# Squares for the residual stream's norms: added over the feature chunks on GpSimd, and one ones-product

## The chip, the cores and the metric

The kernel runs on one core of one Trainium2 chip. The core has TensorE (PE, matrix products into PSUM), VectorE (DVE), ScalarE (ACT) and GpSimd (POOL), which work on SBUF side by side and wait for each other by semaphores, and DMA queues. The metric is device time in microseconds; the kernel before takes 3798.35 us, the median of three runs from 3797.68 to 3798.63.

## The reference

The reference computes three blocks one after the other on 512 latent tokens of 1024 features, beside which the first block has 256 context tokens. The first block has two layers. The change touches these two layers alone, and in them one thing: the mean square in the norms that read the residual stream `x`.

```python
def rmsnorm(u, g):
    uf = u.astype(jnp.float32)
    y = uf * lax.rsqrt(jnp.mean(uf * uf, axis=-1, keepdims=True) + EPS)
    return (y * g.astype(jnp.float32)).astype(u.dtype)
...
        hl = modulate(rmsnorm(xl, g_pre_mix[i]), ml[0], ml[1])
...
        xl_new = xl + ml[2] * rmsnorm(y_l, g_post_mix[i])
        h2 = modulate(rmsnorm(xl_new, g_pre_mlp[i]), ml[3], ml[4])
        xl_new = xl_new + ml[5] * rmsnorm(sqrelu_mlp(h2, w_mlp_in[i], w_mlp_out[i]), g_post_mlp[i])
```

In each layer a mixer (latent attention, a gated convolution, a short convolution) and an MLP add their normed outputs to `x`, and `x` is normed again ahead of the next product. The context goes the same way in the first layer. A second attention block and a layer of experts that are looked up by keys follow; they stay as they are.

## The kernel before

The stream is kept with the features on the partitions: eight chunks of 128 features, each a tile of 128 x 768 columns, 256 of the context (`xc`) and 512 latent (`x`). Weight products are done in three parts (`mm3`, L322), since every fp32 value is split into a high and a low part (`hh`, `hl` for the tokens; `wh` made by ACT in L276 and `wl` by DVE in L277 for the weights). A product's result goes to PSUM in tiles of two kinds: `a` (`acc`, 1024 columns, two of them) and `b` (`acc1`, 512 columns, four of them); the units of `lin` take the two kinds in turn.

A norm needs the mean over the features, which lie on the partitions. A product with a matrix of ones, divided by 1024, gives it on all partitions (`ones_mean`, L345, and L568). An fp32 product is two passes on TensorE. `rstd` (L333 and L334 on ACT, L335 and L336 on DVE) makes the reciprocal root from the PSUM tile, and `prenorm` (L532 on DVE, L533 on ACT, L534 on DVE) makes the normed tokens of each chunk, as `hh` and `hl`, which the next products read.

`chain` adds a normed output to the stream: for each of the eight chunks DVE multiplies (L547) and adds (L550), ACT squares the new `x` (L565) and `meansq_x` adds that square's column sums to the PSUM tile (L568). Then `prenorm` follows, or the sum is kept. `meansq_x` is also called for the input, in `build` and `start`. There are eleven such sums up to 1726 us, each of a range of columns: set 1 (512 columns, the input's first tokens, in `build`), set 2 (256, the input's others, in `start`), sets 3 (512) and 4 (256) behind the mixer of layer 0, sets 5 to 7 (256 each) behind its MLP, and sets 8 and 9 (256 each) and 10 and 11 (256 each) behind the mixer and the MLP of layer 1.

The chains are generators that run in steps beside the products. Beside them the modulation of the layers is computed in groups of 256 columns: L467 multiplies `mraw` or `mg` (from DMA) with `cs` into a `b` tile, ACT copies it to `mrow` (L469), L472 turns it, and L474 and L476 on DVE finish it. The order on each engine is set by a scheduler from the order in which the code is written and the tiles that are taken: a tile of a kind that has been taken later can only come into use behind those taken before it.

Of the kernel before, what the change touches and what calls it, by code (L numbers as in the profile page):

```python
# [5 lines left out]
F32 = mybir.dt.float32  # L6
# [3 lines left out]
OP = mybir.AluOpType  # L10
# [61 lines left out]
TBW = 16  # L72
# [171 lines left out]
class K:  # L244
# [26 lines left out]
    def split(self, raw, shape):  # L271
        """hi, lo of raw"""
        nc = self.nc
        hi = self.t("wh", shape, F32R, NWH, self.wp)
        lo = self.t("wl", shape, F32R, NWH, self.wp)
        nc.scalar.copy(hi, raw)  # L276
        nc.vector.tensor_tensor(lo, raw, hi, op=OP.subtract)  # L277
        return hi, lo
# [6 lines left out]
    def take(self, key, hold=False):  # L285
        """the next weights of the plan, the ones behind them on their way; held ones stay until they are dropped"""
        if not self.ready:
            self.ready.append((self.plan[0][0], self.plan.popleft()[1]()))
        k, w = self.ready.popleft()
        assert k == key, (k, key)  # L290
        self.held += hold
        self.refill(not hold)
        return w
# [5 lines left out]
    def drop(self, w):  # L299
        """a held one that is used for the last time"""  # L300
        self.held -= 1
        self.refill(1)
        return w
# [13 lines left out]
    def mm3(self, outs, w, x, start, stop):  # L317
        """outs: psum aps; w: (hi, lo) stationary; x: per out (hi, lo) moving."""
        nc = self.nc
        for xi, wi in ((0, 0), (1, 0), (0, 1)):  # L320
            for o, xx in zip(outs, x):
                nc.tensor.matmul(o, w[wi], xx[xi], start=start and xi == 0 and wi == 0, stop=stop and wi == 1)  # L322

# [1 line left out]
    def ct(self, tag, w):  # L325
        """a temporary tile of the norms between the parts of a layer"""
        return self.t("PTq", [128, 512], F32, 6)[:, :w]

    def rstd(self, mean_ps, n, t=None):
        """mean_ps: psum [128, n] of mean squares on all partitions; -2 / sqrt of them, to be used with gains times -1/2"""  # L330
        nc = self.nc
        v, y = (t(x, n) if t else self.t(x, [128, T])[:, :n] for x in ("rs_v", "rs_y"))
        nc.scalar.activation(y, mean_ps, AF.Abs_reciprocal_sqrt, bias=self.eps)  # L333
        nc.scalar.activation(v, y, AF.Square)  # L334
        nc.vector.scalar_tensor_tensor(v, mean_ps, EPS, v, op0=OP.add, op1=OP.mult)  # L335
        nc.vector.scalar_tensor_tensor(y, v, 3.0, y, op0=OP.subtract, op1=OP.mult)  # L336
        return y

    def ones_mean(self, src, n, dim):
        """mean over features of src [128, n] (sum over partitions / dim), as psum [128, n]"""  # L340
        p = self.acc1() if n <= 512 else self.acc()
        o = self.ones[dim]
        for a in range(0, n, 512):
            b = min(a + 512, n)
            self.nc.tensor.matmul(p[:, a:b], o, src[:, a:b], start=True, stop=True)  # L345
        return p[:, :n]
# [17 lines left out]
    def setup(self):  # L364
# [4 lines left out]
        # gains times -1/2, the weights of the gated convolution times 1/2  # L369
# [26 lines left out]
    def load_xc(self):  # L396
        """the context's tokens, three feature chunks to a tile"""
        self.xc = []
        for i in range(0, 8, 3):
            t = self.t("xc", [128, T])  # L400
            for k in range(i, min(i + 3, 8)):
                c = t[:, (k - i) * SC:(k - i) * SC + SC]
                self.nc.sync.dma_start(out=c, in_=self.a["cT"][k])
                self.xc.append(c)

    def xa(self, k, c0, c1):
        """columns c0 to c1 of feature chunk k; the context's tokens come first"""
        return self.xc[k][:, c0:c1] if c1 <= SC else self.x[k][:, c0 - SC:c1 - SC]

    def pipe(self, tasks):  # L410
        """tasks in order; a task that yields n goes on behind the n-th task after it"""
# [22 lines left out]
    def adv(self, n=1000):  # L434
        """n steps of the first of the generators that run beside the tasks"""
        while n and self.bg:
            if next(self.bg[0], self) is self:
                self.bg.popleft()
                return
            n -= 1  # L440
# [20 lines left out]
    def mod_group(self, l, g, ws):  # L461
        """columns 256 g to 256 g + 256 of the modulation of layer l"""
# [15 lines left out]
    def mods(self, todo):  # L478
        """closures for the groups (layer, group) of todo; a group's weights are loaded behind the group before it"""

        def step(i):
            ws = self.mw or self.mod_load(*todo[i])
            self.mod_group(*todo[i], ws)
            self.mw = self.mod_load(*todo[i + 1]) if i + 1 < len(todo) else None

        return [lambda i=i: step(i) for i in range(len(todo))]

    def tick(self, upto=1000):
        """one more group of modulations, upto that many in all"""
# [4 lines left out]
    def mod_fold(self, l, j, gname, plus_one, k0, k1):  # L494
        """[128, k1 - k0, 2]: -gain / 2 * (mod_j (+1))"""
# [9 lines left out]
    def fold(self, l, j, gname, plus_one, k):  # L505
        """column of mod_fold for feature chunk k, made for two chunks at a time"""
# [9 lines left out]
    def pieces(self, r):  # L516
        """(stream, first column, last column) of a range of columns"""
        return [(s, max(r[0], a), min(r[1], b)) for s, a, b in ((1, 0, SC), (0, SC, T)) if r[0] < b and r[1] > a]

    def prenorm(self, l, j, gname, mean, hs, rg):  # L520
        """normed and modulated tokens of columns rg as hi, lo; yields after each chunk"""
# [15 lines left out]
    def chain(self, l, j, gname, Y, ssq, nxt, hs, rg):  # L537
        """x += gate * norm(Y) and the norm that follows, on the tokens of columns rg"""
# [19 lines left out]
    def meansq_x(self, p, k, rg):  # L558
        """mean square over the features of the tokens, added up in psum"""
# [3 lines left out]
        s = self.ct("sqt", w)  # L563
        for _, a, b in self.pieces(rg):
            nc.scalar.activation(s[:, a - x0:b - x0], self.xa(k, a, b), AF.Square)  # L565
        if k == 0:
            p = self.acc1()
        nc.tensor.matmul(p[:, :w], self.ones[1024], s, start=k == 0, stop=k == 7)  # L568
        return p if k < 7 else p[:, :w]

    def lin(self, ap, hs, R, w=None, ks=None):
        """products of a tile of 128 columns: one psum tile for each range of R"""
# [18 lines left out]
    def stagger(self, units, hs, stages, n, upto):  # L591
        """units on the ranges of the first stage, then on those of the next ones, with n steps beside each"""
# [12 lines left out]
    def start(self, units, hs):  # L605
        """the first units, on the first tokens as they become ready, then on the others"""
# [32 lines left out]
    def normed_hilo(self, c, r, g, n, dst=None):  # L639
        """c * g * r as hi, lo"""  # L640
# [4 lines left out]
    def layer(self, l, hs):  # L645
# [11 lines left out]
        # ---- conformer branch  # L657
# [66 lines left out]
        # ---- short convolution branch  # L724
# [43 lines left out]
        # ---- latents, keys and queries  # L768
# [73 lines left out]
        def k_pair(i):  # L842
            """keys of heads 2 i and 2 i + 1: the second one's rows lie the other way round"""
# [30 lines left out]
        # ---- attention of two heads on a block of 128 queries  # L874
# [62 lines left out]
        # ---- output projection  # L937
# [28 lines left out]
        # the first units run on the tokens that are ready  # L966
# [36 lines left out]
        # ---- mlp  # L1003
# [77 lines left out]
    def norm2(self, gname, X, mean):  # L1081
        """normed tokens as hi, lo, from the mean squares in psum of each range of columns"""
# [25 lines left out]
    def stackq(self, out, z, e, w=slice(0, S)):  # L1108
        """head e of z: hi on its own rows of out, lo on the other ones"""
# [4 lines left out]
    def stackk(self, z):  # L1114
        """each head of z twice on top of itself"""
# [6 lines left out]
    def mm64(self, out, q, k, stop=True):  # L1122
        """q: hi and lo of 64 rows on top of each other; k: hi twice, lo twice"""
# [13 lines left out]
    def lin2k(self, key, hs, wide=False):  # L1137
        """products of the plan's next tile of weights"""
# [7 lines left out]
    def block2(self):  # L1146
# [10 lines left out]
        # the halves of the rotary rows change places here; the other rows stay zero  # L1157
# [4 lines left out]
        def rope_unit(j, gi, done):  # L1162
            """a tile of 128 columns (two heads): norm, gain and rotary, then done"""
# [45 lines left out]
        # ---- values and gates, token-major  # L1209
# [29 lines left out]
        # ---- compressed keys and values  # L1239
# [112 lines left out]
        # ---- selected and window branches: head pair i (heads i and 4 + i) on query block qb  # L1352
# [18 lines left out]
        def out(key, qb, Y, tag):  # L1371
            """psum of the pair of query blocks of qb, and a copy of it behind the second"""
# [50 lines left out]
        # ---- dilated attention: head pair jp on query block qb  # L1423
# [86 lines left out]
        # ---- merge  # L1510
# [56 lines left out]
        at = {}  # L1567
# [32 lines left out]
    def peer(self, hs):  # L1600
# [44 lines left out]
        def route(b):  # L1645
            """experts and weights of token block b, pairs on partitions; yields the vector engine's ns"""
# [29 lines left out]
            # row and column of the candidate  # L1676
# [34 lines left out]
        def weights(tb, share):  # L1711
            """expert weights of TBW tokens; each share-th group of four on the vector engine only"""
# [27 lines left out]
        def routing():  # L1740
            """expert weights of a token block beside the routing of the next one; yields the ns on the vector and the scalar engine"""
# [59 lines left out]
    def build(self, upto=None):  # L1801
# [18 lines left out]
        def feed(i):  # L1820
            """modulation and norm of the first tokens for two more chunks of features"""
# [48 lines left out]
```

## Time and profile before

| | |
|---|---|
| median of three runs | 3798.35 us (3797.68 to 3798.63) |
| profiled execution, span | 3799.5 us, 52788 instructions; the page gives no other time for it |
| TensorE busy | 3700.0 us, 97% |
| VectorE, ScalarE busy | 2464.8 us (65%), 1749.5 us (46%) |
| GpSimd busy | 159.3 us, 4%, most of it in the last third |

The page gives busy time for each engine, the clock that TensorE was granted, and the chain of work that ended last, followed back from the last instruction. The groups by line give busy time, the mean of one in ns, and the idle time ahead of them with what ended it. The timeline and the table by stretch give the same for any stretch. A pair of passes that stands in a full queue is drawn longer than it costs, because the ends of products are modelled; what it costs is the distance to the next start.

### The profile page before, as it was taken

The numbers are of one execution on the slowest core, as the hardware profiler recorded it, in microseconds if no ns is written. First come the engines' busy times: TensorE is split into PE (matmuls) and PEld (weight loads), VectorE is DVE, ScalarE is ACT, GpSimd is POOL, SyncE is SP. The second block draws the span as 40 slices with busy tenths as digits, with TensorE's granted clock in tenths as the row PEclk, the third lists the DMA queues.
The fourth block names the chain that finished last, engine by engine and source line by source line (L and its number), as shares of the span: only waits on it lengthen the run. The fifth ranks groups of instructions, "written<-read, shape, count | busy, mean of one in ns | idle before, by whom it ended". The sixth has DMA issues, their size and how long they took to land.

```text
span 3799.5 us, 52788 instructions
## 1 busy us (share of the span) xinstructions
PE 3700.0 (97%) x19762; PEld 3052.0 (80%) x19762; DVE 2464.8 (65%) x4950; ACT 1749.5 (46%) x3452; POOL 159.3 (4%) x317
## 2 busy tenths in 40 slices
PE   8998999999999999999999999999999999999999
PEld 5867788888877878887778878778888888888887
DVE  5966644444788655555776568999666855555554
ACT  5256531111446732233565544767777743322232
POOL 0000000000000000000001100000000011111110
PEclk9999999999999999999999999999999999999999
DMA  6430331222341233334331233455555565665553
GB/s 209 129 106 12 122 117 62 61 66 63 105 147 51 67 117 95 94 97 138 115 99 62 93 111 106 156 168 176 178 178 178 195 218 189 201 205 187 190 186 114
DMA packets 155248, 490.28 MB, mean 129 GB/s; under 512 B 18368, under 2 KB 24832, under 8 KB 150768
## 3 DMA queue, kind: packets, MB, share of 16 engines
q1 hardware_dynamic: 128368, 374.48, 30.9%
q0 software_dynamic: 26624, 112.43, 8.7%
q8 instruction: 156, 2.56, 0.3%
q14 instruction: 100, 0.82, 0.1%
HBM read 408.86 MB, written 74.71 MB: 127 GB/s over the span
## 4 chain that ended last, share of the span: by engine, by line
PE 85%; DVE 9%; ACT 2%; DMA 2%; issue 1%; SPq 0%; POOL 0%; ACTq 0%; DVEq 0%; POOLq 0%
PE b L322 56%; PE a L322 19%; PE b L917 2%; DVE wl L277 1%; PE b L467 1%; PE a L1732 1%; PE b L568 1%; PE b L906 1%; PE b L1419 1%; PE b L1365 1%; DMA mraw<-in_wmod_dram 1%; DVE gst L1736 1%; PE a L1125 0%; PE b L1507 0%; PE b L1174 0%
## 5 line engine op out<-in xcount | busy, mean ns | idle before, releaser
L276 ACT CAST wh<-raw 128x1024 fp32r<-128x1024 f32 (+2 forms) x531 | 547.3, 1031 | 1365.7 <-PE b L322 811.3
L322 PE MATMUL b<-hs,wh 128*128 128x512 f32 x2624 | 823.6, 395 | 4.4 <-ACT hs L1092 4.4
L277 DVE TENSOR_TENSOR wl<-raw,wh 128x1024 fp32r<-128x1024 f32 (+2 forms) x531 | 635.7, 1198 | 171.7 <-ACT wh L276 159.1
L322 PE MATMUL b<-hid,wh 128*128 128x512 f32 x2048 | 630.7, 389 | 0.0
L322 PEld LDWEIGHTS b<-hs,wh 128*128 128x128 f32 x2624 | 487.5, 190 | 107.7 <-ACT hs L1092 5.3
L322 PE MATMUL b<-hs,wl 128*128 128x512 f32 x1312 | 516.2, 393 | 1.1 <-DVE wl L277 1.1
L322 PEld LDWEIGHTS b<-hid,wh 128*128 128x128 f32 x2048 | 384.4, 188 | 80.2 <-DVE hid L1795 0.3
L322 PE MATMUL b<-hid,wl 128*128 128x512 f32 x1024 | 398.3, 389 | 0.0
L322 PE MATMUL b<-hh,wh 128*128 128x256 f32 (+1 forms) x1160 | 364.7, 351 | 3.7 <-DVE V L840 2.2
L322 PE MATMUL a<-hh,wh 128*128 128x512 f32 (+1 forms) x1144 | 354.7, 348 | 9.5 <-DVE y L1046 7.2
L322 PE MATMUL b<-hl,wh 128*128 128x256 f32 (+1 forms) x1160 | 356.3, 344 | 0.3 <-DVE hl L534 0.3
L322 PE MATMUL b<-hh,wl 128*128 128x256 f32 (+1 forms) x1160 | 355.7, 344 | 0.0
L322 PE MATMUL a<-hh,wl 128*128 128x512 f32 (+1 forms) x1144 | 350.2, 344 | 1.5 <-DVE wl L277 1.5
L322 PE MATMUL a<-hl,wh 128*128 128x512 f32 (+1 forms) x1144 | 349.9, 343 | 0.3 <-DVE hl L534 0.3
L322 PEld LDWEIGHTS b<-hs,wl 128*128 128x128 f32 x1312 | 248.4, 189 | 53.7 <-DVE wl L277 1.5
L322 PEld LDWEIGHTS b<-hh,wh 128*128 128x128 f32 x1160 | 200.5, 189 | 44.0 <-issue 4.7
L322 PEld LDWEIGHTS a<-hh,wh 128*128 128x128 f32 x1144 | 197.0, 188 | 44.3 <-issue 14.0
L322 PEld LDWEIGHTS b<-hl,wh 128*128 128x128 f32 x1160 | 201.0, 189 | 30.5 <-issue 1.2
L322 PEld LDWEIGHTS b<-hid,wl 128*128 128x128 f32 x1024 | 192.2, 188 | 39.9
L322 PEld LDWEIGHTS a<-hl,wh 128*128 128x128 f32 x1144 | 197.3, 188 | 31.8 <-issue 2.5
L322 PEld LDWEIGHTS b<-hh,wl 128*128 128x128 f32 x1160 | 200.4, 189 | 27.7 <-issue 1.1
L322 PEld LDWEIGHTS a<-hh,wl 128*128 128x128 f32 x1144 | 196.9, 188 | 30.3 <-DVE wl L277 2.3
(412 smaller groups left out, 5424.1 us busy)
## 6 DMA issues: line engine op xcount, KB each, us to landing
raw<-in_w_dram SPq DMA_DIRECT2D x134, 512.0 KB
raw<-in_pu_dram SPq DMA_DIRECT2D x128, 512.0 KB
raw<-in_pv_dram SPq DMA_DIRECT2D x128, 512.0 KB
raw<-in_win_dram SPq DMA_DIRECT2D x64, 512.0 KB
G<-gst POOLq DMA_DIRECT2D x32, 1024.0 KB, 4.9
gt<-G POOLq DMA_DIRECT2D x16, 2048.0 KB, 13.9
mraw<-in_wmod_dram SPq DMA_DIRECT2D x82, 384.0 KB
GA<-ga SPq DMA_DIRECT2D x121, 256.0 KB
```

The costliest lines, as they stand in the source:

```text
L276: nc.scalar.copy(hi, raw)
L277: nc.vector.tensor_tensor(lo, raw, hi, op=OP.subtract)
L322: nc.tensor.matmul(o, w[wi], xx[xi], start=start and xi == 0 and wi == 0, stop=stop and wi == 1)
L467: nc.tensor.matmul(p[j:j + 32, 0:256], self.cs[:, k, :], ws[k], start=k < 4, stop=k >= 4, tile_position=(0, j))
L568: nc.tensor.matmul(p[:, :w], self.ones[1024], s, start=k == 0, stop=k == 7)
L906: nc.tensor.transpose(p[:, j * 128:j * 128 + 128], Ps[e][:, kc * 128:kc * 128 + 128], self.eye)
L917: nc.tensor.matmul(o[pr, c % 2 * 128:c % 2 * 128 + 128], V[i][:, kc, pr], PT[e * nkb + kc], start=kc == 0, stop=kc == nkb - 1, tile_positi ...
L1365: nc.tensor.transpose(p[:, j * 128:j * 128 + 128], src, self.eye)
L1419: nc.tensor.matmul(o[row], V[kb][:, 128 * b + 64 * g:128 * b + 64 * g + 64], PT[kb][2 * g + b], start=False, stop=kb == qb and b == 1, til ...
L1732: nc.tensor.matmul(p[:, i * 256:i * 256 + 256], A[:, i], W[:, i].rearrange("p j e -> p (j e)"), start=True, stop=True)
L1736: nc.vector.tensor_tensor(gst[:, :, t8:t8 + 4].rearrange("p e t -> p t e"), q[:, :, 0], lo, op=OP.add)
```

## The change

`meansq_x` no longer sends each square to TensorE. The square of chunk 0 is written to a new tile, `msq` (two of them in SBUF), and stays there. The squares of chunks 1 to 7 are written as before and GpSimd adds each to `msq`. Behind the last one `ones_mean` takes a PSUM tile and multiplies `msq` with the ones once. The callers are as they were. (The diff also takes out docstrings and comments, which are left out here.)

```diff
-    def meansq_x(self, p, k, rg):
+    def meansq_x(self, acc, k, rg):
         nc = self.nc
         x0, x1 = rg
         w = x1 - x0
-        s = self.ct("sqt", w)
+        s = self.t("msq", [128, 512], F32, 2)[:, :w] if k == 0 else self.ct("sqt", w)
         for _, a, b in self.pieces(rg):
             nc.scalar.activation(s[:, a - x0:b - x0], self.xa(k, a, b), AF.Square)
         if k == 0:
-            p = self.acc1()
-        nc.tensor.matmul(p[:, :w], self.ones[1024], s, start=k == 0, stop=k == 7)
-        return p if k < 7 else p[:, :w]
+            return s
+        nc.gpsimd.tensor_tensor(acc, acc, s, op=OP.add)
+        return acc if k < 7 else self.ones_mean(acc, w, 1024)
```

The 88 products of L568 (176 passes) become eleven of L345 (22 passes), and GpSimd gets 77 additions, 63 of 256 columns and 14 of 512. In the changed kernel the additions have the line L568.

The order of TensorE in set 9 before, from the end of an `a` unit on; `b_12352` is the sum, `b_12460` a modulation group, `b_12481` a unit of 24 products:

```order
L322 MATMUL a_12550<-hh_10607,wl_12383 128x256
L568 MATMUL b_12352<-PTq_12350,ones_77 128x256
L467 MATMUL b_12460<-mraw_12333,cs 32x256 x3
L322 MATMUL b_12481<-hh_11541,wh_12260 128x256
L322 MATMUL b_12481<-hl_11542,wh_12260 128x256
L568 MATMUL b_12352<-PTq_12357,ones_77 128x256
L467 MATMUL b_12460<-mraw_12335,cs 32x256 x3
L568 MATMUL b_12352<-PTq_12363,ones_77 128x256
L467 MATMUL b_12460<-mraw_12337,cs 32x256 x2
L322 MATMUL b_12481<-hh_11541,wl_12261 128x256
L322 MATMUL b_12481<-hh_11547,wh_12260 128x256
```

The same place now; `b_12444` is the sum:

```order
L322 MATMUL a_12550<-hh_10607,wl_12381 128x256
L345 MATMUL b_12444<-msq_12350,ones_77 128x256
L467 MATMUL b_12460<-mraw_12333,cs 32x256 x3
L467 MATMUL b_12460<-mraw_12335,cs 32x256 x3
L467 MATMUL b_12460<-mraw_12337,cs 32x256 x2
L322 MATMUL b_12481<-hh_11541,wh_12260 128x256
L322 MATMUL b_12481<-hl_11542,wh_12260 128x256
L322 MATMUL b_12481<-hh_11541,wl_12261 128x256
L322 MATMUL b_12481<-hh_11547,wh_12260 128x256
```

The one product of the sum stands where the first of eight stood, and the modulation group and the unit, which stood between the eight, stand behind it. Set 4 has the same form.

VectorE in set 9 before, from chunk 5 on; L474 and L476 finish the modulation group `b_12460`, L335 reads the sum:

```order
L547 TENSOR_TENSOR PTq_12428<-y_11803,PTq_12342 128x256
L474 TENSOR_REDUCE mod_118<-b_12460 128x4
L550 SCALAR_TENSOR_TENSOR x_103<-PTq_12428,mf_12014,x_103 128x256
L476 TENSOR_TENSOR mod_118<-mod_118,vec 128x4
L547 TENSOR_TENSOR PTq_12434<-y_11843,PTq_12342 128x256
L502 TENSOR_TENSOR mf_15016<-mod_118,vecn 128x4
L550 SCALAR_TENSOR_TENSOR x_104<-PTq_12434,mf_12063,x_104 128x256
L547 TENSOR_TENSOR PTq_12440<-y_11883,PTq_12342 128x256
L550 SCALAR_TENSOR_TENSOR x_105<-PTq_12440,mf_12063,x_105 128x256
L1012 TENSOR_SCALAR pn_t_12506<-b_12481 128x256
L335 SCALAR_TENSOR_TENSOR PTq_12446<-b_12352,PTq_12446 128x256
```

The same place now, from chunk 6 on:

```order
L547 TENSOR_TENSOR PTq_12432<-y_11843,PTq_12342 128x256
L550 SCALAR_TENSOR_TENSOR x_104<-PTq_12432,mf_12061,x_104 128x256
L547 TENSOR_TENSOR PTq_12438<-y_11883,PTq_12342 128x256
L550 SCALAR_TENSOR_TENSOR x_105<-PTq_12438,mf_12061,x_105 128x256
L335 SCALAR_TENSOR_TENSOR PTq_12446<-b_12444,PTq_12446 128x256
L336 SCALAR_TENSOR_TENSOR PTq_12447<-PTq_12446,PTq_12447 128x256
L532 SCALAR_TENSOR_TENSOR PTq_12452<-x_98,mf_12117,PTq_12447 128x256
L532 SCALAR_TENSOR_TENSOR PTq_12456<-x_99,mf_12117,PTq_12447 128x256
L532 SCALAR_TENSOR_TENSOR PTq_12511<-x_100,mf_12162,PTq_12447 128x256
L534 SCALAR_TENSOR_TENSOR hl_11542<-PTq_12452,mod_118,hh_11541 128x256
L534 SCALAR_TENSOR_TENSOR hl_11548<-PTq_12456,mod_118,hh_11547 128x256
L474 TENSOR_REDUCE mod_118<-b_12460 128x4
```

The reduction L474, which stood between the chunks of the set, stands behind L335, L336 and the first steps of the prenorm.

## Rows read from the trace of the kernel before

**Rows 1.** Page: busy time by engine, and the chain by line.

```profile
PE 3700.0 (97%) x19762; PEld 3052.0 (80%) x19762; DVE 2464.8 (65%) x4950; ACT 1749.5 (46%) x3452; POOL 159.3 (4%) x317
...
PE b L322 56%; PE a L322 19%; PE b L917 2%; DVE wl L277 1%; PE b L467 1%; PE a L1732 1%; PE b L568 1%; PE b L906 1%; PE b L1419 1%; PE b L1365 1%; DMA mraw<-in_wmod_dram 1%; DVE gst L1736 1%; PE a L1125 0%; PE b L1507 0%; PE b L1174 0%
```

**Rows 2.** Groups by line on TensorE, 0 to 1730 us; columns as in part 5.

```profile
L568 PE MATMUL b<-PTq,ones 128*128 128x256 f32 (+1 forms) x176 | 65.5, 478 | 16.3 <-ACT PTq L565 16.1
```

**Rows 3.** Table by stretch, L568 alone: length, busy us (passes) of TensorE, weight loads, clock.

```profile
10.00:20.00 10.00, 9.27 (x16) 3.75 (x16) 1.00 0.98 316
...
1700.00:1713.00 13.00, 3.82 (x12) 1.80 (x12) 1.00 0.26 82
```

**Rows 4.** Timeline of set 9: start, us, engine, line, operation [idle before <- releaser].

```profile
1345.51 0.70 PE L568 MATMUL b<-PTq,ones 128*128 128x256 f32 x2
...
1350.82 0.17 DVE L474 TENSOR_REDUCE mod<-b 128x4 f32<-128x16 f32 x1 [1.77 <-PE b L472]
...
1353.26 0.42 ACT L565 ACTIVATE PTq<-x 128x256 f32<-128x256 f32 x1 [0.44 <-DVE x L550]
...
1353.77 0.28 PE L322 MATMUL b<-hl,wh 128*128 128x256 f32 x1
...
1353.89 0.59 PE L568 MATMUL b<-PTq,ones 128*128 128x256 f32 x2
...
1354.13 0.47 PE L322 MATMUL b<-hh,wl 128*128 128x256 f32 x1
...
1354.43 0.28 PE L322 MATMUL b<-hh,wh 128*128 128x256 f32 x1
...
1354.52 0.47 ACT L333 ACTIVATE PTq<-b,eps 128x256 f32<-128x256 f32 x1 [0.84 <-PE b L568]
...
1356.44 0.44 PE L472 MATMUL b<-cst,mrow 128*128 128x128 f32 x2 [0.49 <-ACT mrow L469]
...
1357.68 0.38 PE L322 MATMUL b<-hh,wh 128*128 128x256 f32 x1 [0.80 <-ACT hh L533]
```

**Rows 5.** L547 and L550 on VectorE: duration ns min/median/max, first and last start.

```profile
L547 DVE TENSOR_TENSOR PTq<-y,PTq x72: 415/419/689, 424.0 to 1724.4; 128x256 f32<-128x256 f32 x64, 128x512 f32<-128x512 f32 x8
...
L550 DVE SCALAR_TENSOR_TENSOR x<-PTq,mf,x x64: 474/483/489, 425.1 to 1724.8; 128x256 f32<-128x256 f32 x64
```

**Rows 6.** Timeline, TensorE ahead of set 6.

```profile
1022.01 0.55 PE L322 MATMUL a<-hh,wh 128*128 128x256 f32 x1 [7.24 <-DVE y L1046]
```

**Rows 7.** Table by stretch behind that idle time; the granted clock stands after POOL.

```profile
1022.00:1024.00 2.00, 1.99 (x7) 1.75 (x7) 1.93 (x6) 0.84 (x2) 0.00 (x0) 0.50 0.09 37
1024.00:1026.00 2.00, 2.00 (x12) 1.81 (x12) 1.93 (x5) 0.84 (x2) 0.00 (x0) 0.71 0.00 0
```

**Rows 8.** Groups by shape on GpSimd, two memsets.

```profile
L1160 POOL MEMSET rot<- 128x512 f32 x4 | 1.9, 543 | 0.0
...
L393 POOL MEMSET cs<- 128x256 f32 x1 | 0.3, 330 | 0.0
```

**Rows 9.** Timeline, sets 4 and 11.

```profile
466.99 0.59 PE L568 MATMUL b<-PTq,ones 128*128 128x256 f32 x2
...
471.17 0.17 DVE L474 TENSOR_REDUCE mod<-b 128x4 f32<-128x16 f32 x1 [1.58 <-PE b L472]
...
475.13 0.59 PE L568 MATMUL b<-PTq,ones 128*128 128x256 f32 x2
...
1725.89 0.70 PE L568 MATMUL b<-PTq,ones 128*128 128x256 f32 x2 [0.16 <-ACT PTq L565]
```

**Rows 10.** Chain of waits in sets 1 and 2: start us, us, what.

```profile
16.54 8.81 DMA mg<-in_wmod_dram
...
52.32 3.63 PE b L568 x16
```

**Rows 11.** Timeline of VectorE in set 4, and beside GpSimd's memsets.

```profile
477.64 1.28 DVE L532 SCALAR_TENSOR_TENSOR PTq<-x,mf,PTq 128x256 f32<-128x256 f32 x3
...
1728.50 1.28 DVE L1091 SCALAR_TENSOR_TENSOR t<-x,vecn,ry 128x256 f32<-128x256 f32 x3
```


## The prediction

> **What bounds the kernel now.** I read the page first. TensorE is busy for 97% of the span and the chain that ended last is made of weight products: L322 has 75% of it, and the lines that the change removes, L568, have 1%, about 38 us [rows 1]. Then the groups by line up to 1730 us, after which the change touches nothing: L568 is 176 matmul passes, 65.5 us, a mean of 478 ns, with 16.3 us of idle ahead of them, nearly all for ACT's squares [rows 2]. (The longest of these waits is that for the first square at the start of the kernel.) Eighty-eight pairs are eleven sums of eight, which I call sets 1 to 11 in order of time. The table by stretch gives a set 3.8 to 9.3 us of TensorE; the largest and the smallest of its eleven rows stand in the group [rows 3]. Last I read one set, number 9, row by row [rows 4], and then the prices.
>
> What a pair costs TensorE is read in set 9. Its last pair starts at 1353.89, the next product at 1354.13 and the one behind it at 1354.43, where a product without a pair behind it takes 0.12 us, as the one at 1353.77 does: 1354.43 - 1353.89 - 0.12 = 0.42 us [rows 4]. The change removes seven of eight pairs, 7 x 0.42 = 2.9 us of a set of 256 columns.
>
> **What the change does to the order.** This is the part that I think decides. Before, the sum's PSUM tile `b` is taken at chunk 0, and the eight pairs stand between other work in `b` tiles, so TensorE does that work while DVE and ACT make the next square. After, the tile is taken at the end. All later `b` tiles stand behind it, and the one L345 pair stands where the first of the eight stood, ahead of the modulation group L467 and the unit `b_12481`. TensorE comes to it when chunk 0 is done and has to wait for chunk 7 and its add. The work that filled that time comes afterwards.
>
> Set 9, worked out. TensorE reaches the sum at 1345.51, as the `a` unit ahead stands where it stood [rows 4]. The last square starts at 1353.26 and lasts 0.42 us, so it ends at 1353.68 [rows 4, 5]. DVE's reduction L474 waited 1.77 us for TensorE in the middle of the set, and goes behind the set in the new order: 1353.68 - 1.77 = 1351.9 [rows 4]. Add one addition (0.76, below): 1352.7. The stall is 1352.7 - 1345.5 = 7.2 us, against 2.9 us saved: +4.3. Some of it comes back: the norm behind the sum (L333) starts at 1352.9 in place of 1354.5, 1.6 us earlier, and runs beside the displaced products, where before TensorE idled 0.49 us ahead of L472 and 0.80 us for L533 [rows 4]; I count 1.6 + 1.3 less 0.1 as coming back. Net +1.5.
>
> The clock comes on top. TensorE's granted clock fell to half (1.2 of 2.4 GHz) while it idled 7.24 us before 1022.01, stood at 0.50 from 1022 to 1024 and at 0.71 from 1024 to 1026 [rows 6, 7]. That is 2 x 0.5 + 2 x 0.29 = 1.6 us lost behind an idle time as long as set 9's stall. Set 9: +1.5 + 1.6 = +3.1.
>
> **An addition on GpSimd.** No two-input GpSimd operation is in this trace. The near rows are memsets: 330 ns for 128x256 and 543 ns for 128x512 [rows 8]. They write only. The difference, 0.213 us, goes to 256 columns, and 0.330 - 0.213 = 0.117 is fixed. An addition reads two and writes one; with three accesses one after another it takes 0.117 + 3 x 0.213 = 0.76 us for 256 and 0.117 + 6 x 0.213 = 1.40 for 512. Bounds are one memset (0.33, 0.54) and three (0.99, 1.63). I take 0.76 and 1.40. DVE's pair of operations sets the pace of a set of 256 columns, 0.42 + 0.48 = 0.90 us of busy time [rows 5], so at 0.76 GpSimd keeps up and only the last addition shows. At 0.99 it would fall behind: some 1.1 us more in each of six sets, +6.6. At 0.33: -0.4 x 6 = -2.4.
>
> The Trainium skill, GPSIMD Engine Reference, section 3.1 Elementwise — side-by-side cycle accounting, gives about 2.6 cycles an element for a two-input add, which would be about 0.6 us at 256 columns; no row here shows one. By it the sum would be about 2 us lower.
>
> **The other sets.** Set 4: the first pair is at 466.99, the last at 475.13, and L474 cost DVE 1.58 us in between [rows 9]. Six products of 512 columns that stood behind the first pair now stand ahead, 1.4 us at about 0.23 us each. TensorE waits from 468.4 to 475.13 - 1.58 + 0.76 = 474.3, 5.9 us, against 2.9 saved; 1 us comes back through the earlier norm: +2.0. Set 7 has the same form with a stall of about 4.5 us: +1.2. Sets 5, 6, 8 and 10: a whole `a` unit is pulled ahead of the sum, so the wait is about what is saved: 0 each, +-2. Set 11: nothing stands beside it; the chain is DVE, ACT, pair, and the last pair is at 1725.89 [rows 9]. The last addition with its hop comes into the chain in place of nothing: +0.9. Set 3: DVE is the engine that paces; the last addition of 1.40 goes on its chain, less what ACT's queue cost there: +1.2. Set 2: squares straight from the input, no DVE work; sixteen passes take 3.63 us of the chain [rows 10], and seven additions of 0.76 take 5.3. The prenorm behind it is on the chain, so +1.5. Set 1: a load of the modulation weights ends at 25.35, well behind the sum [rows 10]; the additions, and a first-use delay of some us if there is one, hide there: 0.
>
> Sum: 0 + 1.5 + 1.2 + 2.0 + 0 + 0 + 1.2 + 0 + 3.1 + 0 + 0.9 = +9.9 us.
>
> **DVE beside the additions.** Three L1091 that run beside L1160's memsets take 1.28 us, as three L532 of the same shape do with GpSimd still [rows 11]. That is for a GpSimd that reads nothing. The lower bound is 0. The upper bound is that each addition keeps DVE's two-input operations out for its whole length: 7 x 0.76 = 5.3 us in each of sets 4, 6, 7, 9 and 11 and 7 x 1.40 = 9.8 in set 3, 36 us. I take a clash of one addition in seven, 5 x 0.76 + 1.40 = 5.2 us, near the row.
>
> Total +15.1 on the profiled span of 3799.5 us, so 3814.6; that span is 1.15 us over the median of the timed runs, 3798.35, so 3813 us. Between the extremes of the near terms (add at 0.33 with no clash; add at 0.99) it runs from 3803 to 3824.
>
> **Rivals.**
> *DVE is kept out.* Each addition starts as its square lands, just as DVE runs its next pair of two-input operations, so they always meet, and the one that comes second waits for the whole of the other. With the upper end of 36 us that is 3799.5 + 9.9 + 36 - 1.15 = 3844; with two thirds of it (24), as some additions fall into DVE's own waits, 3832. Against it: the memset rows. For it: no row shows a reading GpSimd beside DVE. It decides if L547 and L550 grow beyond 0.6 us in sets 3 to 11. The Trainium skill, SBUF — State Buffer, section "Who interferes with whom", states this rule: a DVE instruction with two SBUF inputs contends with a GpSimd instruction that reads SBUF, and the loser waits for the whole instruction. The rows of before neither show nor exclude it, since their GpSimd operations only write; this is why I give it over 0.2.
>
> *TensorE gains.* If the waits at the sum are short, because TensorE comes to it late or other work is found, seven sets of 256 columns (4 to 10) give 7 x 2.9 = 20 us: 3778; half of it 3788. For it: TensorE is busy 97% [rows 1], and L568 waits rarely outside the start. Against it: the order of sets 4 and 9, which I can read.
>
> *A wash.* Stalls equal what is saved and the additions hide: 3796 to 3803. It needs the displaced work to cover the norm behind the sum wholly, in every set.
>
> **Chances.** Forecast 0.50 (3803 to 3824), DVE kept out 0.22, TensorE gains 0.15, a wash 0.13. A measurement of this kernel tells about 0.2% from no change, 7.6 us, so faster is under 3790.8 and slower over 3806. Faster: most of the gain, 0.13. Same: the wash, the rest of the gain and the low end of the forecast, 0.24. Slower: 0.63. The range runs from half the TensorE gain, which it leaves out, to most of the DVE case: 3791 to 3838.
>
> **What would show it.** In the new trace L345 of sets 4, 7 and 9 has idle of 4 to 8 us ahead of it, released by GpSimd's `msq`, and TensorE's busy time to 1730 us is about 55 us lower with the same or a later end. The granted clock behind set 9 falls. Additions take 0.6 to 0.9 us. L547 and L550 stay at 0.42 and 0.48 but for single longer ones; if most are longer, the second price was wrong and the first rival holds. If the waits ahead of L345 are under 2 us, the order argument is wrong.

## The result and the profile after

The changed kernel takes 3846.67 us, the median of four runs (3844.03 to 3849.45), beside 3798.01 us for the kernel before: a ratio of 1.0127, 95% interval 1.0113 to 1.0142. It is 49 us slower. 3813 was forecast and 3838 was the end of the range.

The page of the kernel after, its span, its busy times and the chain by line:

```profile
span 3847.6 us, 52630 instructions
...
PE 3664.8 (95%) x19608; PEld 3029.0 (79%) x19608; DVE 2487.7 (65%) x4950; ACT 1755.0 (46%) x3454; POOL 241.6 (6%) x394
...
PE b L322 55%; PE a L322 18%; PE b L917 2%; DVE wl L277 1%; PE b L467 1%; PE a L1732 1%; PE b L906 1%; PE b L1419 1%; DVE PTq L547 1%; DVE x L550 1%; PE b L1365 1%; DMA mraw<-in_wmod_dram 1%; PE b L345 1%; POOL msq L568 1%; PE b L1507 1%
```

TensorE is busy for 35 us less than before, 3664.8 against 3700.0 [rows 1], and the span is 48.1 us longer. L568 and L345 alone do not stand for that in the chain: VectorE's L547 and L550, which were not among its costly lines before, have 1% each now.

TensorE's waits up to 1790 us (in total, times, the longest):

```profile
PE b L345 <- POOL msq L568: 84.2, 11, 18.9
PE a L322 <- DVE wl L277: 21.0, 3, 10.5
```

The first is the pair of the sum, eleven waits. The one at the start of the kernel is 18.9 us, where the first wait was 10.4 before; the other ten make 65 us. The second is nearly new (1.5 us before): weight halves that VectorE makes later than before.

The additions, and the two operations of VectorE that make the new stream, by shape (busy us, mean ns of one):

```profile
L568 POOL TENSOR_TENSOR msq<-msq,PTq 128x256 f32<-128x256 f32 x63 | 59.3, 941 | 1200.5 <-ACT PTq L565 1199.0
...
L568 POOL TENSOR_TENSOR msq<-msq,PTq 128x512 f32<-128x512 f32 x14 | 22.9, 1634 | 229.7 <-ACT PTq L565 229.2
```

```profile
L550 DVE SCALAR_TENSOR_TENSOR x<-PTq,mf,x 128x256 f32<-128x256 f32 x64 | 40.2, 634 | 0.7
...
L547 DVE TENSOR_TENSOR PTq<-y,PTq 128x256 f32<-128x256 f32 x64 | 33.4, 529 | 0.1
...
L550 DVE SCALAR_TENSOR_TENSOR xc<-PTq,mf,xc 128x256 f32<-128x256 f32 x16 | 13.9, 874 | 0.2
```

An addition of 256 columns takes 0.94 us on average. The mean of L550 has gone from 482 to 634 ns, and from 483 to 874 for the context's chunks, that of L547 from 419 to 529 ([rows 5] has the durations of before). The median of L550 on `x` stays at 484 ns: 24 of the 64 took more than 600 ns, and most of the others are as before. How this looks is best seen in set 9, on all engines (start, us, engine, line, operation):

```profile
1380.35 0.72 POOL L568 TENSOR_TENSOR msq<-msq,PTq 128x256 f32<-128x256 f32 x1 [1.01 <-ACT PTq L565]
1380.47 0.89 DVE L550 SCALAR_TENSOR_TENSOR x<-PTq,mf,x 128x256 f32<-128x256 f32 x1
...
1381.95 1.71 POOL L568 TENSOR_TENSOR msq<-msq,PTq 128x256 f32<-128x256 f32 x2 [0.87 <-ACT PTq L565]
1382.13 0.95 DVE L547 TENSOR_TENSOR PTq<-y,PTq 128x256 f32<-128x256 f32 x1
...
1383.12 0.83 DVE L550 SCALAR_TENSOR_TENSOR x<-PTq,mf,x 128x256 f32<-128x256 f32 x1
...
1386.62 0.42 ACT L565 ACTIVATE PTq<-x 128x256 f32<-128x256 f32 x1 [1.31 <-DVE x L550]
1387.18 0.72 POOL L568 TENSOR_TENSOR msq<-msq,PTq 128x256 f32<-128x256 f32 x1 [0.93 <-ACT PTq L565]
1387.95 1.22 PE L345 MATMUL b<-msq,ones 128*128 128x256 f32 x2 [9.33 <-POOL msq L568]
1389.10 1.94 PE L467 MATMUL b<-mraw,cs 128*32 128x256 f32 x16
1389.21 0.47 ACT L333 ACTIVATE PTq<-b,eps 128x256 f32<-128x256 f32 x1 [2.17 <-PE b L345]
```

The addition of 1380.35 takes 0.72 us, and L550, which was issued inside it, takes 0.89 and ends 0.29 us behind it. So 0.19 of its 0.48 us had passed when the addition was over, if it ran on at its usual pace; whether this is its own start or part of its work, no run shows. At 1381.95 two additions stand beside L547 at 0.95 us and L550 at 0.83, which are lengthened too. TensorE waits 9.33 us for the last addition and starts the pair 0.77 us after that addition began. Before, the first pair of this set started without a wait [rows 4]. The stretches around it (length, busy us of the engines, then TensorE's granted clock):

```profile
1384.00:1388.00 4.00, 0.05 (x1) 0.05 (x1) 2.46 (x4) 1.23 (x3) 2.35 (x3) 0.50 0.00 0
1388.00:1392.00 4.00, 4.00 (x26) 2.02 (x27) 1.69 (x5) 1.58 (x4) 0.00 (x0) 0.63 0.18 36
```

The clock was 0.50, half of full speed (1.2 of 2.4 GHz), at the end of the wait, and 0.63 over the next 4 us. It is not set 9 alone. Over the stretch up to 1790 us, before and after, the means (after POOL) are:

```profile
0.00:1790.00 1790.00, 1719.70 (x10262) 1413.25 (x10262) 1093.44 (x2077) 708.41 (x1260) 15.64 (x63) 0.98 0.31 98
...
0.00:1790.00 1790.00, 1635.62 (x9708) 1347.85 (x9709) 1099.49 (x2052) 701.13 (x1246) 92.87 (x128) 0.96 0.30 94
```

By the clock's records in the two traces it stood at 0.50 for 58 us of this stretch before and for 130 us after; TensorE was busy in 45 and in 65 us of these.

Where the 48 us came from, by the start of L333 (or of the DMA behind set 11) in both traces:

| behind | before | after | later by | of it in this stretch | forecast, without the 5.2 us of clashes |
|---|---|---|---|---|---|
| sets 1, 2 | 420.17 | 423.45 | 3.3 | 3.3 | 1.5 |
| sets 3, 4 | 992.29 | 1013.55 | 21.3 | 18.0 | 3.2 |
| sets 5 to 7 | 1103.99 | 1138.47 | 34.5 | 13.2 | 1.2 |
| (no set) | 1306.11 | 1338.73 | 32.6 | -1.9 | 0 |
| sets 8, 9 | 1698.32 | 1738.25 | 39.9 | 7.3 | 3.1 |
| sets 10, 11 | 1727.14 | 1775.46 | 48.3 | 8.4 | 0.9 |

Every group lost more than was forecast, sets 3 and 4, where the additions have 512 and 256 columns, the most.

### The profile page after: what moved, and what is told of

The parts are those of the page before. It is cut to its first block, busy times and chain, and to the rows that moved or that the text cites. A ratio compares the mean times of both kernels' runs of the same rounds, so it can differ in the third digit from the quotient of the medians.

```text
span 3847.6 us, 52630 instructions
## 1 busy us (share of the span) xinstructions
PE 3664.8 (95%) x19608; PEld 3029.0 (79%) x19608; DVE 2487.7 (65%) x4950; ACT 1755.0 (46%) x3454; POOL 241.6 (6%) x394
## 4 chain that ended last, share of the span: by engine, by line
PE 84%; DVE 10%; ACT 3%; DMA 2%; issue 1%; POOL 1%; SPq 0%; ACTq 0%; DVEq 0%; POOLq 0%
PE b L322 55%; PE a L322 18%; PE b L917 2%; DVE wl L277 1%; PE b L467 1%; PE a L1732 1%; PE b L906 1%; PE b L1419 1%; DVE PTq L547 1%; DVE x L550 1%; PE b L1365 1%; DMA mraw<-in_wmod_dram 1%; PE b L345 1%; POOL msq L568 1%; PE b L1507 1%
```

## The experiments

Four causes were to be told apart: the place of the pair in TensorE's queue (ORDER), VectorE kept out by GpSimd's additions (PORT), the time and delay that additions bring whoever makes them (LENGTH), and, against all, the gain on TensorE. Ratios are to the kernel before on the same chip, with their 95% interval; differences in us are those of medians. The kernels were not all timed on one chip, so a difference between two of them that stand beside different runs of the kernel before is less sure than a ratio.

**Pairs left out, the tile opened at chunk 0.**

```diff
-        nc.tensor.matmul(p[:, :w], self.ones[1024], s, start=k == 0, stop=k == 7)
+        if k in (0, 7):
+            nc.tensor.matmul(p[:, :w], self.ones[1024], s, start=k == 0, stop=k == 7)
```

> The squares of chunks 1 to 6 are left out of the sum; chunk 0's pair opens the tile and chunk 7's closes it, no additions. The products stand as in the kernel with six additions behind an opened tile. It shows what 66 pairs fewer on TensorE are worth with nothing added. If TensorE paces these stages: 66 x 0.42 = 28 us less, 3770. If the pairs ran in time in which TensorE waited for VectorE anyway: 3788 to 3798. LENGTH expects about 25 us between this and the kernel with additions on VectorE.

3799.83 us against 3797.43, ratio 1.0005 (0.9996 to 1.0015), a little over the range. Sixty-six pairs fewer and no gain. TensorE's busy time up to 1730 us (second number) and its waits say why:

```profile
0.00:1730.00 1730.00, 1633.37 (x9663) 1342.12 (x9664) 1066.32 (x2027) 692.79 (x1232) 10.23 (x49) 0.98 0.30 96
```

```profile
PE b L569 <- ACT PTq L565: 33.1, 14, 10.8
PE b L322 <- ACT hh L533: 9.8, 3, 4.3
...
PE a L322 <- ACT hh L533: 5.5, 5, 2.3
```

Up to 1730 us TensorE is busy for 1633.4 us, where the kernel before has 1660.7: 27 us less, as 66 x 0.42 said. It has become waiting, for squares (33.1 us, 16.1 before) and for the norm's first chunks (15.3, 1.8 before). So the pairs had filled time that TensorE otherwise waits. A part went into the clock: it stands at 0.50 for 89 us up to 1790 us, and TensorE is busy in 61 us of these (58 and 45 before), an estimated 8 us of products at half speed that stand inside the 1633. A kernel whose clock stays up might have kept some of the gain; no run tells.

**The same squares left out, the pair in its early place.**

```diff
-        if k == 0:
-            p = self.acc1()
-        nc.tensor.matmul(p[:, :w], self.ones[1024], s, start=k == 0, stop=k == 7)
-        return p if k < 7 else p[:, :w]
+        return s if k < 7 else self.ones_mean(s, w, 1024)
```

> The squares of chunks 0 to 6 are made and left out of the sum; the one pair takes chunk 7's square alone, and stands in TensorE's queue where the changed kernel's pair stands. It is the changed kernel without any addition. ORDER (the early place of the pair is a cost of its own): 3805 to 3825, TensorE idle 3 to 9 us ahead of the pair in sets 4, 7, 9, 10, 11. LENGTH (what costs is the time that additions add to VectorE's and the sum's chain, by keeping VectorE out or by standing behind the square): 3780 to 3798.

3810.49 us, ratio 1.0033 (1.0020 to 1.0045). TensorE's order is that of the changed kernel but for a few products, without an addition. The pair of set 9 in it:

```profile
1356.64 1.22 PE L345 MATMUL b<-PTq,ones 128*128 128x256 f32 x2 [5.87 <-ACT PTq L565]
```

5.87 us of waiting. The place costs 3810.5 - 3799.8 = 10.7 us by itself (5 to 17 by the two intervals), with VectorE's work as it was, though in another order. ORDER holds, as one part of 49.

**Additions on GpSimd, the tile opened at chunk 0.**

```diff
+        s = self.t("msq", ...) if k == 1 else self.ct("sqt", w)
...
+        if k == 0:
+            p = self.acc1()
+            nc.tensor.matmul(p[:, :w], self.ones[1024], s, start=True, stop=False)
+            return p, None
+        p, acc = p
+        if k == 1:
+            return p, s
+        nc.gpsimd.tensor_tensor(acc, acc, s, op=OP.add)
...
+        nc.tensor.matmul(p[:, :w], self.ones[1024], acc, start=False, stop=True)
```

> GpSimd still adds (six additions a set), but the square of chunk 0 goes to PSUM at once, so the sum's tile is open from chunk 0 and the closing pair stands behind the modulation group and the unit that the change had pushed behind it. Theory ORDER (TensorE waits at a pair that stands too early): the waits at the closing pair shrink from 73 us to under 20, time 3785 to 3808. Theory PORT (additions keep DVE's two-input operations out, the order matters little): the additions cost as before, time 3820 to 3845.

3832.81 us against 3797.13, ratio 1.0091 (1.0074 to 1.0108). The closing pair (L576) stands behind the modulation group and the unit again; L568 is the opening pair here:

```profile
PE b L576 <- POOL msq L573: 33.2, 11, 9.3
PE b L568 <- ACT PTq L565: 21.3, 7, 9.1
```

Both together wait 54.5 us, against 84.2 for the changed kernel's pair and 16.1 for the pairs of before, and the kernel is still 36 us slower. PORT's range was met and ORDER's, in time and in waits, was not.

**Additions on VectorE**, in both places; one word of the diff above, and of the change:

```diff
-        nc.gpsimd.tensor_tensor(acc, acc, s, op=OP.add)
+        nc.vector.tensor_tensor(acc, acc, s, op=OP.add)
```

> Both undone: the tile opened at chunk 0 and six additions a set on VectorE. ORDER and PORT both expect no loss: TensorE saves six pairs of 0.42 us a set, VectorE has 2.5 us more a set, time 3775 to 3802. A third theory, that the added length of the chain itself (an addition between square and sum) costs, whoever adds: 3810 to 3830.

> The changed kernel with its 77 additions on VectorE instead of GpSimd; the pair stands as early as in the changed kernel. ORDER: the wait at the pair stays 5 to 12 us a set and VectorE has 7 x 0.42 us more a set, time 3830 to 3850. PORT: nothing is kept out any more, time 3798 to 3815.

The opened tile: 3824.22 us, ratio 1.0076 (1.0059 to 1.0093). The early pair: 3833.11 us, 1.0093 (1.0076 to 1.0109). Both theories had expected no loss of the first; it is 27 us, so LENGTH was needed. The second lies in ORDER's range and not in PORT's. The waits of the first on TensorE:

```profile
PE b L568 <- ACT PTq L565: 26.7, 9, 9.7
PE b L576 <- DVE msq L573: 12.7, 5, 7.3
PE b L322 <- ACT hh L533: 11.5, 3, 4.3
```

Against the kernels that leave the additions out, VectorE's additions cost 24 us with the opened tile (3824.2 - 3799.8) and 23 in the early place (3833.1 - 3810.5).

**Additions beside, nobody waits for them**, on GpSimd and on VectorE; all pairs stay:

```diff
         nc.tensor.matmul(p[:, :w], self.ones[1024], s, start=k == 0, stop=k == 7)
+        if k:
+            d = self.t("msq", [128, 512], F32, 2)[:, :w]
+            nc.gpsimd.tensor_tensor(d, s, s, op=OP.add)     # nc.vector in the other
```

> The kernel before with all its 88 pairs on TensorE, and beside them 77 additions on GpSimd of each square to itself, into a tile that nobody reads. PORT: every addition keeps DVE out for its 0.7 us as in the changed kernel, time 3815 to 3835. ORDER: the products stand as before, VectorE has slack, time 3798 to 3808. L550 and L547 up to 1.5 us in either case.

> The kernel before with all its pairs, and 77 additions on VectorE of each square to itself into a tile that nobody reads: VectorE has 63 x 0.42 + 14 x 0.69 = 36 us more work, nothing waits for its result. If the 24 us of additions on VectorE in the sum are VectorE's time (the stages are paced by it): 3815 to 3826. If they are the delay between square and pair (nobody waits here): 3798 to 3805.

On GpSimd 3813.56 us against 3797.13, ratio 1.0037 (1.0023 to 1.0051): 16 us, between the two ranges and near PORT's, with TensorE's order as before and no result awaited. On VectorE 3819.91 against 3796.04, 1.0065 (1.0048 to 1.0081): 24 us, as much as when the sum waits for them. The pages' busy times, first beside GpSimd's additions, then with VectorE's:

```profile
PE 3703.8 (97%) x19762; PEld 3051.7 (80%) x19762; DVE 2483.4 (65%) x4950; ACT 1750.9 (46%) x3452; POOL 220.6 (6%) x394
...
PE 3710.3 (97%) x19762; PEld 3054.6 (80%) x19762; DVE 2492.0 (65%) x5027; ACT 1752.4 (46%) x3454; POOL 159.6 (4%) x317
```

VectorE is busy for 19 and 27 us more than before (2464.8), and the kernels are 16 and 24 us longer. So what is added to VectorE's busy time here comes out nearly whole in the kernel's time: VectorE paces these stages, and the delay behind the square is not what counts. GpSimd's additions and VectorE's operations beside them, by shape:

```profile
L571 POOL TENSOR_TENSOR msq<-PTq 128x256 f32<-128x256 f32 x63 | 46.1, 735 | 1185.1 <-ACT PTq L565 1184.4
...
L571 POOL TENSOR_TENSOR msq<-PTq 128x512 f32<-128x512 f32 x14 | 15.5, 1121 | 233.5 <-ACT PTq L565 233.5
```

```profile
L550 DVE SCALAR_TENSOR_TENSOR x<-PTq,mf,x 128x256 f32<-128x256 f32 x64 | 35.3, 551 | 1.2
...
L547 DVE TENSOR_TENSOR PTq<-y,PTq 128x256 f32<-128x256 f32 x64 | 32.0, 500 | 0.2
```

L550 is at 551 ns (482 before) and L547 at 500 (419), although nothing has been added to VectorE. By the starts and ends in this trace, 33 of the 64 L550 on `x` met an addition and took 621 ns on average; the 31 that met none took 478. The additions take 735 ns here (they add a square to itself; in the changed kernel 941).

**Writes beside**, two memsets of each square's tile behind its pair:

```diff
+        if k:
+            for _ in range(2):
+                nc.gpsimd.memset(s, 0.0)
```

> The kernel before with all its pairs, and beside them on GpSimd two memsets of each square's tile behind its pair (chunks 1 to 7), which write as long as an addition lasts and read nothing. If only a reading GpSimd keeps VectorE out: 3796 to 3801, L547 and L550 at 0.42 and 0.48 us. If any GpSimd work beside VectorE costs: 3808 to 3816, as with the additions beside (3814).

3802.36 us, ratio 1.0007 (0.9997 to 1.0016): no difference that can be told, a little over the range. VectorE's two lines:

```profile
L550 DVE SCALAR_TENSOR_TENSOR x<-PTq,mf,x 128x256 f32<-128x256 f32 x64 | 30.8, 482 | 1.2
...
L547 DVE TENSOR_TENSOR PTq<-y,PTq 128x256 f32<-128x256 f32 x64 | 26.8, 419 | 0.2
```

482 and 419 ns, to the nanosecond those of before. The memsets come later than the additions did, behind the pair, but they met VectorE as often: 31 of the 64 L550 ran beside one, and took 482 ns like the others. It is the reading GpSimd that keeps VectorE out.

**Chunk 7 past GpSimd.** As the opened tile with GpSimd's additions, but the last square goes to TensorE directly:

```diff
+        if k < 7:
+            nc.gpsimd.tensor_tensor(acc, acc, s, op=OP.add)
+            return p, acc
+        nc.tensor.matmul(p[:, :w], self.ones[1024], acc, start=False, stop=False)
+        nc.tensor.matmul(p[:, :w], self.ones[1024], s, start=False, stop=True)
```

> GpSimd adds the squares of chunks 2 to 6 onto that of chunk 1 (five additions a set); chunk 0 opens the tile on TensorE, chunk 7's square goes to TensorE directly and closes it. Against the opened tile with six additions, one addition and its hop are gone from behind the last square. If GpSimd's cost beyond keeping VectorE out (33 against 16 us) is the tail behind the last square: 11 x (0.7 to 1.2) = 8 to 13 us less, 3819 to 3825. If it is the pace of the additions along the whole set: 3828 to 3833.

3822.33 us against 3796.04, ratio 1.0066 (1.0049 to 1.0082): 26 us slower, against 36 with the addition in place. The addition behind the last square was worth about 10 us, 0.9 in each set; by the two intervals, on different chips, it may be anything from just over 0 to 19. That there are eleven additions fewer to keep VectorE out does not explain it: VectorE is busy for 2483.2 us here and for 2484.0 with them. TensorE's waits at the closing pair fell less, from 33.2 to 28.8 us.

**One pass for two**, squares and ones as fp32r:

```diff
-        s = self.ct("sqt", w)
+        s = self.t("PTq", [128, 512], F32R, 6)[:, :w]
...
+        nc.tensor.matmul(p[:, :w], self.onesr, s, start=k == 0, stop=k == 7)
```

> The kernel before, with the squares written and multiplied as fp32r in place of fp32, so that each product is one pass. 88 passes fewer. If TensorE paces: 88 x 0.2 to 0.3 us less, 3772 to 3780. If its pairs were covered: 3790 to 3798. Nothing is slower by either theory.

3800.49 us, ratio 1.0005 (0.9995 to 1.0014), a little over the range. Less TensorE time in these sums gives nothing, a second time; here too the clock stands at 0.50 for 89 us up to 1790 us.

**The change turned round**, in search of a better kernel: VectorE's additions of the outputs' squares (L360) as pairs on TensorE, in fp32, and in fp32r with one pass.

```diff
+    def sumsq_pe(self, acc, c, n):
+        p, i = acc or (self.acc1(), 0)
...
+        nc.scalar.activation(s, c, AF.Square)
+        nc.tensor.matmul(p[:, :n], self.ones[1024], s, start=i == 0, stop=i == 7)
+        return p, i + 1
```

> The change turned round: the kernel before with the squares of the mixer's and the MLP's outputs, which VectorE adds up in 63 additions (L360, 0.42 us each, 0.69 at 512 columns, some 28 us) for nine sums, sent to TensorE pair by pair as L568 does. If VectorE paces these stages as it does the eleven sets: 3775 to 3790. If TensorE's products pace there, because they run while the units of the output projection and the MLP do: 3800 to 3820, as 63 more pairs of 0.42 us are 26 us of TensorE.

> The same with all these squares and those of the residual stream as fp32r, one pass for each product. VectorE paces: 3770 to 3788. TensorE paces: 3795 to 3808, as a pass costs about half a pair.

3843.62 us, ratio 1.0119 (1.0102 to 1.0136), and 3825.54 us, 1.0072 (1.0055 to 1.0089). Both missed, on the dear side. The page's busy times of the first and of the second, and the first's new passes:

```profile
PE 3745.7 (97%) x19888; PEld 3082.2 (80%) x19888; DVE 2444.4 (64%) x4887; ACT 1752.3 (46%) x3452; POOL 159.3 (4%) x317
...
PE 3701.6 (97%) x19728; PEld 3054.9 (80%) x19728; DVE 2446.7 (64%) x4888; ACT 1752.1 (46%) x3452; POOL 159.8 (4%) x317
```

```profile
L359 PE MATMUL b<-PTq,ones 128*128 128x256 f32 (+1 forms) x144 | 49.4, 432 | 3.5 <-ACT PTq L358 3.4
```

In the first TensorE's busy time is 45.7 us over that of before, and its idle time (span less busy time) is 101.4 us, 99.5 before: the loss is busy time. The new passes are drawn with 49.4 us. So TensorE paces there, as the units of the output projection and of the MLP run beside. A pair of the kind that was free beside `chain` costs its full time a stage earlier: by starts in this trace, 22 of 28 pairs of 256 columns between products of the units take 0.59 to 0.70 us. The second is another case: TensorE's busy time is only 1.6 us over that of before, and its loss is idle time (126.5 us in all), whose cause was not followed up. No version beat the kernel before.

## Why the prediction was wrong

It had the sign right, and less than a third of the size: +15 against +49. Its 15.1 are 4.0 for the place of the pair with its credit and the clock, 5.9 for additions that show behind the squares, and 5.2 for clashes on VectorE. The runs give 13 for the first (3810.5 - 3797.4), about 10 for the second and 16 for the third, and 10 are left over. The clash is the largest miss, the credit the next.

**The credit.** The step that failed first is "5.9 us, against 2.9 saved", "+4.3" and the zeros of sets 5, 6, 8 and 10: each stall was set off against seven pairs at 0.42 us. The price of a pair was near (27 us less busy, forecast 28 for 66, with some 8 us of half speed in it), but it was a price on TensorE's queue, and it bought nothing: with the pairs left out the time stays, at 1.0005. Busy time would not have told this: in the twelve us of set 9 before, TensorE is busy for 11.27 and VectorE for 8.18:

```profile
1345.00:1349.00 4.00, 3.98 (x27) 1.86 (x27) 3.90 (x12) 1.71 (x5) 0.00 (x0) 1.00 0.71 199
1349.00:1353.00 4.00, 3.90 (x27) 3.17 (x24) 2.20 (x9) 1.53 (x4) 0.00 (x0) 1.00 0.57 206
1353.00:1357.00 4.00, 3.39 (x32) 2.25 (x30) 2.08 (x7) 1.99 (x5) 0.00 (x0) 1.00 0.02 4
```

A pair priced in a full queue does not show whether the queue would be as long without it. The rival that TensorE gains had this wrong altogether.

**VectorE beside the additions.** "I take a clash of one addition in seven, 5 x 0.76 + 1.40 = 5.2 us, near the row": measured 16 us by itself, with every pair in place. The row taken was a memset's [rows 8, 11], which only writes, and the run with memsets shows that such a row says nothing of an operation that reads. The rival "DVE is kept out" had the mechanism and its place, and 3832 to 3844 for the time; it was given 0.22. It got that time in part by luck, as the place of the pair and the last additions are in the 49 us too. Its sign, most of L547 and L550 beyond 0.6 us, was not met: 24 of the 64 L550 on `x` are (mean 634 ns, median 484). Those that met an addition are longer, and the others are not. The rule of the Trainium skill (SBUF — State Buffer, "Who interferes with whom"), that an instruction of VectorE with two SBUF inputs contends with a GpSimd instruction that reads SBUF and not with one that only writes, agrees with both runs: 551 against 482 ns for L550 beside additions, 482 beside memsets. That the loser waits for the whole of the other, as the rival had it, the L550 at 1380.47 does not bear out to the full: it ended 0.29 us behind the addition and not 0.48.

**The additions.** 0.76 us was taken for 256 columns and 1.40 for 512. For an addition by itself that was near: 11 and 7 additions ran with VectorE idle, and took 0.72 and 1.26 us. The other 52 and 7 took 0.99 and 2.01 on average, so VectorE keeps GpSimd out too, and the means over all are 0.94 and 1.63. The upper bounds, 0.99 and 1.63, were the better values here. The range of the near terms, 3803 to 3824, does not follow from them: the additions at 0.33 without a clash give 3806, those at 0.99 give 3820. The Trainium skill (GPSIMD Engine Reference, section 3.1) gives about 0.6 us by its 2.6 cycles an element; with 0.72 at least, the measurement decides. Behind the last square an addition was worth about 0.9 us in each set; the forecast had it for set 11, set 3 and in the stalls, and nothing in sets 5, 6, 8 and 10.

**The order.** This step held. The pair stands early and TensorE waits at it: 9.3 us in set 9 (7.2 forecast), 7.9 in set 4 (5.9), 8.8 in set 7 (4.5). By itself the place costs 10.7 us. The reason given was that the tile is taken late; its first product comes late as well, the opened kernels do both at chunk 0, and no run tells the two apart. Sets 10 and 11 were missed; there TensorE waits 10.9 and 12.8 us.

**The clock.** It fell behind set 9 as forecast (0.50 at the end of the wait), and the 1.6 us were of the right size: 4 x 0.37 = 1.5 in the 4 us behind it. But it was put at nothing in all other sets. With 20 us more of busy time at 0.50 than before, the estimate is 10 us up to 1790 us and not 1.6. It is spread over the parts below, as the kernels without additions have 6 and 8 us of it.

The parts, measured apart: place 10.7, VectorE kept out 16, the last addition about 10, and 2 for the pairs left out, no difference that can be told. That makes 39 of 49. The other 10 us were not measured apart. The early place costs 14 us with the additions on GpSimd (3846.7 - 3832.8) against 10.7 without, and VectorE's busy time has grown by 23 us in the changed kernel (2487.7), against 19 beside the additions that nobody waits for. How far these two make up the 10 stays open.

## What to carry to other kernels

Work that one engine does between other engines' results may be free, however long its queue makes it look: leave it out in a run and see whether the time moves, before it is moved to another engine. An accumulation that was done piece by piece, between other work, became a point where the queue stood still when it was turned into one product at the end. And an elementwise operation on GpSimd that reads SBUF was not off VectorE's path where VectorE's operations read two tensors from SBUF.

## What the runs showed of the hardware

L550 in the kernel after, by duration in ns (min/median/max) and first and last start:

```profile
L550 DVE SCALAR_TENSOR_TENSOR x<-PTq,mf,x x64: 470/484/1511, 428.9 to 1771.7; 128x256 f32<-128x256 f32 x64
```

A GpSimd that reads lengthened VectorE's operations with two SBUF inputs at 256 columns, up to 1511 ns for one of 470 to 484; 154 memsets beside them did not lengthen them by a nanosecond in the mean. An fp32 addition of two tiles takes GpSimd 0.72 us at 256 columns and 1.26 at 512 with VectorE idle, where VectorE takes 0.42 and 0.69; of a tile to itself GpSimd's shortest take 0.61 and 1.03. Pairs of passes that were free beside the chain cost 0.7 us each a stage earlier (45.7 us of busy time for 63 more pairs, seven of them of 512 columns), where TensorE sets the pace. And leaving out 66 of the pairs kept TensorE's clock at 0.50 for 89 us in place of 58.
